# A Mamba-2 layer's convolution of x with tokens on partitions: shifted copies by DMA in place of TensorE transposes

## The chip, the cores and the metric

The kernel runs on one core of a Trainium2 chip. The metric is the device time of one execution in microseconds. A core has five engines that each work through their own instructions in order: TensorE (PE; its weight loads are listed apart as PEld), VectorE (DVE), ScalarE (ACT), GpSimd (POOL) and SyncE (SP), which here issues nearly all transfers. The transfers themselves are moved by 16 DMA engines. [...]

## The reference

The reference is a decoder trunk of two layers on 256 tokens with a width of 2048, all in float32. Layer 0 mixes tokens by latent attention (MLA), layer 1 by a state-space mixer (SSM, Mamba-2); behind each stands an MLP with a squared ReLU, 2048 to 8192 to 2048, and everything is added to the residual. The change touches the SSM mixer only, whose core is this:

```python
z, xbc, dt = jnp.split(h @ w_in, [...])            # 4096, 6144, 64 columns
xbc = silu(conv_w[0]*xbc[s-3] + conv_w[1]*xbc[s-2] + conv_w[2]*xbc[s-1] + conv_w[3]*xbc[s] + conv_b)
xs, b_in, c_in = split(xbc, [4096, 1024, 1024])    # 8 groups: x 512, B 128, C 128 columns each
# per group: cb = C B^T (256 x 256, causal); per head of 64 columns (8 heads a group):
#   y = (cb * decay(dt, head)) @ (x * dt) + d_skip * x
y = rms_norm_per_group(y * silu(z)) * norm_g
return y @ w_out                                   # 4096 to 2048
```

The convolution runs along the tokens: each column's value at token s takes the column's own values at s, s-1, s-2 and s-3 (zero before the first token), each with a weight of that column, and a bias of that column.

## The kernel before

**Products and weight units.** All large products have tokens on the output's partitions: two accumulators (tokens 0 to 127 and 128 to 255) of 512 columns in PSUM. float32 is carried as a high and a low half, and a product takes three passes. Weights stream from HBM in *units* of 128 x 1024 (512 KB): SP loads one into one of six `raw` buffers (`fetch`, L87), ScalarE makes its high half `wh` (L102), VectorE the low half `wl` (L103), four buffers each, and TensorE runs eight products with `wh` (L325, L326) and four with `wl` (L329) in `block`. `Flow.next` loads six units ahead of the one in use and converts three ahead. A *key* is two units, a *block* of the SSM layer four keys, that is 8 units, and gives 512 columns for all 256 tokens.

**Order.** TensorE's instructions stand in the order in which the program writes them. The other engines' instructions are put in order by the tile framework, which knows the waits and sets each where it expects it to be ready. At the end of each key `tick` runs the small steps that `later(n, fn)` put off by n ticks; so transposes, group products and gates fall between keys. The SSM layer's blocks come as B0, dt, B1, C0, C1 and then as `SSM_ORDER` says: x blocks (one per group), z blocks, and blocks o of the output product.

**Convolution before.** The accumulators of an x, B or C block have tokens on partitions. `conv` first copies them to SBUF (`evac`, ScalarE L1093), turns them by TensorE transposes so that columns lie on partitions and tokens along the free axis (L1070), and there a shift in time is a shifted slice: ScalarE multiplies by the last tap and adds the bias (L1076), VectorE adds the three other taps (L1079), ScalarE takes a tanh (L1081), VectorE ends the SiLU (L1082). B and C stay in that layout, which their products want. x has to come back: `back` (in `x_block`) transposes it again (L1179) and ScalarE copies it out (L1181) to `xtm`, tokens on partitions. Per x group that is 8 transposes there and 8 back.

**After the convolution.** `cb_group` makes cb (L1156 to L1161), `head` loads a broadcast row of cumulated decays (L1215, SP) and makes a head's factor on ScalarE and VectorE (L1219 to L1222); eight heads later `products` multiplies them with x (L1237), `across` adds the first half's part to the second (L1195, L1197), and the z block's `gate` (L1262 to L1276) finishes the group.

**Buffers.** All of it lies in SBUF: `xtm` six tiles, `cb` one per group, `mt` (head factors) eleven, scratch `s2` seven. GpSimd's transfers that add while they write (L199, in the MLPs only) use a scratch area for their descriptors, of the framework's default size.

## Time and profile before

| | |
|---|---|
| median of 3 runs | 2308.71 us (2308.22 to 2309.93) |
| span of the profiled execution | 2306.1 us; no other time of that execution is given, the median of the runs stands 2.6 us above it |
| TensorE busy | 2298.4 us |
| VectorE busy | 1890.2 us |
| ScalarE busy | 1419.4 us |
| GpSimd busy | 187.9 us |
| granted TensorE clock | full in all slices |
| read from HBM | 506.58 MB, 221 GB/s over the span |

How to read it: busy time is the time in which an engine had an instruction of its own under way; "x" is a count; a group's row gives its line, engine, operation, the tiles written and read, shapes, count, busy time, the mean duration of one in ns, and then the idle time of the engine ahead of these instructions with what ended it. TensorE's products overlap, so that one lasts 390 ns while they start closer together. SPq and POOLq are the queues that issue transfers; the time to landing runs from the issue to the arrival of the whole transfer.

### The profile page before, as it was taken

The numbers are of one execution on the slowest core, as the hardware profiler recorded it, in microseconds if no ns is written. First come the engines' busy times: TensorE is split into PE (matmuls) and PEld (weight loads), VectorE is DVE, ScalarE is ACT, GpSimd is POOL, SyncE is SP. The second block draws the span as 40 slices with busy tenths as digits, with TensorE's granted clock in tenths as the row PEclk, the third lists the DMA queues.
The fourth block names the chain that finished last, engine by engine and source line by source line (L and its number), as shares of the span: only waits on it lengthen the run. The fifth ranks groups of instructions, "written<-read, shape, count | busy, mean of one in ns | idle before, by whom it ended". The sixth has DMA issues, their size and how long they took to land.

```text
span 2306.1 us, 30756 instructions
## 1 busy us (share of the span) xinstructions
PE 2298.4 (100%) x11057; PEld 1911.1 (83%) x11057; DVE 1890.2 (82%) x2318; ACT 1419.4 (62%) x1995; POOL 187.9 (8%) x227
## 2 busy tenths in 40 slices
PE   9999999999999999999999999999999999999999
PEld 7888888888888888888888888888888888888887
DVE  7786697999899897678788767756989989989895
ACT  7775466566666656575577555545666656666663
POOL 1430000000000000000022001110000000000000
PEclk9999999999999999999999999999999999999999
DMA  8444677877887877665566656556687788787874
GB/s 316 148 129 155 200 233 245 262 239 250 265 243 247 267 217 241 198 211 180 169 204 207 223 181 204 186 191 201 201 257 234 250 265 250 241 268 240 250 230 161
DMA packets 152153, 510.77 MB, mean 221 GB/s; under 512 B 17152, under 2 KB 26304, under 8 KB 152000
## 3 DMA queue, kind: packets, MB, share of 16 engines
q1 hardware_dynamic: 143712, 479.37, 62.7%
q0 software_dynamic: 8064, 29.36, 7.6%
q8 instruction: 87, 1.43, 0.3%
q14 instruction: 66, 0.54, 0.1%
q10 hardware_dynamic: 224, 0.07, 0.0%
HBM read 506.58 MB, written 2.16 MB: 221 GB/s over the span
## 4 chain that ended last, share of the span: by engine, by line
PE 98%; DMA 1%; DVE 0%; ACT 0%; issue 0%; SPq 0%; POOL 0%; DVEq 0%; ACTq 0%
PE acc L325 13%; PE acc L326 13%; PE acc L329 13%; PE yp L595 9%; PE yp L596 9%; PE yp L594 9%; PE st L595 8%; PE st L596 8%; PE st L594 8%; PE sm L310 2%; PE y L1237 1%; PE acc L596 1%; PE acc L595 1%; PE acc L594 1%; PE acc L703 0%; DMA wraw<-mi 0%
## 5 line engine op out<-in xcount | busy, mean ns | idle before, releaser
L102 ACT ACTIVATE wh<-wraw 128x1024 fp32r<-128x1024 f32 (+1 forms) x818 | 860.0, 1054 | 627.6 <-PE acc L326 311.0
L103 DVE TENSOR_TENSOR wl<-wraw,wh 128x1024 fp32r<-128x1024 f32 (+1 forms) x818 | 987.9, 1220 | 265.1 <-ACT wh L102 255.0
L594 PE MATMUL yp<-wh,k 128*128 128x512 f32 x896 | 349.8, 390 | 0.0
L595 PE MATMUL yp<-wl,k 128*128 128x512 f32 x896 | 348.9, 389 | 0.5 <-DVE wl L103 0.4
L596 PE MATMUL yp<-wh,k 128*128 128x512 f32 x896 | 348.8, 389 | 0.0
L325 PE MATMUL acc<-wh,xt 128*128 128x512 f32 x704 | 280.8, 399 | 1.3 <-ACT wh L102 1.3
L326 PE MATMUL acc<-wh,xt 128*128 128x512 f32 x704 | 274.6, 390 | 0.0
L102 ACT ACTIVATE wh<-wrx 128x1024 fp32r<-128x1024 f32 x168 | 177.9, 1059 | 136.3 <-PE yp L596 108.0
L103 DVE TENSOR_TENSOR wl<-wrx,wh 128x1024 fp32r<-128x1024 f32 x168 | 204.0, 1219 | 38.5 <-ACT wh L102 38.3
L595 PEld LDWEIGHTS yp<-wl,k 128*128 128x128 f32 x896 | 168.2, 188 | 36.0 <-DVE wl L103 1.4
L596 PEld LDWEIGHTS yp<-wh,k 128*128 128x128 f32 x896 | 168.2, 188 | 35.0
L594 PEld LDWEIGHTS yp<-wh,k 128*128 128x128 f32 x896 | 168.2, 188 | 34.6
L325 PE MATMUL acc<-wh,k 128*128 128x512 f32 x496 | 196.7, 397 | 0.0
L326 PE MATMUL acc<-wh,k 128*128 128x512 f32 x496 | 193.3, 390 | 0.0
L329 PE MATMUL acc<-wl,xt 128*128 128x512 f32 x704 | 188.4, 389 | 0.0
L594 PE MATMUL st<-wh,xt 128*128 128x512 f32 x448 | 176.8, 395 | 0.0
L595 PE MATMUL st<-wl,xt 128*128 128x512 f32 x448 | 174.8, 390 | 0.0
L596 PE MATMUL st<-wh,xt 128*128 128x512 f32 x448 | 174.8, 390 | 0.0
L325 PEld LDWEIGHTS acc<-wh,xt 128*128 128x128 f32 x704 | 132.3, 188 | 29.7 <-ACT wh L102 2.8
L329 PEld LDWEIGHTS acc<-wl,xt 128*128 128x128 f32 x704 | 132.1, 188 | 27.9
L326 PEld LDWEIGHTS acc<-wh,xt 128*128 128x128 f32 x704 | 132.3, 188 | 26.9 <-issue 1.0
L199 POOL DMA_DIRECT2D wrx<-mi x56 | 48.8, 872 | 1140.3 <-DVE wl L103 1034.3
(302 smaller groups left out, 3458.8 us busy)
## 6 DMA issues: line engine op xcount, KB each, us to landing
wraw<-mi SPq DMA_DIRECT2D x256, 512.0 KB, 5.2
wraw<-mo SPq DMA_DIRECT2D x256, 512.0 KB, 5.3
wraw<-si SPq DMA_DIRECT2D x160, 512.0 KB, 4.5
wraw<-so SPq DMA_DIRECT2D x64, 512.0 KB, 4.3
wrx<-mi SPq DMA_DIRECT2D x56, 512.0 KB, 5.0
wrx<-mi POOLq DMA_DIRECT2D x56, 512.0 KB, 8.1
wraw<-wo SPq DMA_DIRECT2D x32, 512.0 KB, 3.8
wraw<-ukv SPq DMA_DIRECT2D x16, 512.0 KB, 4.1
```

The costliest lines, as they stand in the source:

```text
L102: self.last = nc.scalar.activation(h[:, v], raw[:, v], AF.Copy)
L103: nc.vector.tensor_tensor(lo[:, v], raw[:, v], h[:, v].bitcast(F32), ALU.subtract)
L199: nc.gpsimd.dma_start(st["b11"].tile, quarter(d, 1, 0), accum_op=ALU.add)
L310: self.nc.tensor.transpose(b[:, j * P:(j + 1) * P], src[:, j * P:(j + 1) * P], self.ident)
L325: nc.tensor.matmul(accs[t][:, :n], ah, wh[:, q, :], start=first and kt + q == 0, stop=False)
L326: nc.tensor.matmul(accs[t][:, :n], al, wh[:, q, :], start=False, stop=False)
L329: nc.tensor.matmul(accs[t][:, :n], lhs(kt + q, t)[0], wl[:, q, :], start=False, stop=en and q == nk - 1)
L594: nc.tensor.matmul(b, ah, wh, start=first and q == 0, stop=False)
L595: nc.tensor.matmul(b, ah, wl, start=False, stop=False)
L596: nc.tensor.matmul(b, al, wh, start=False, stop=last and q == 1)
L1237: nc.tensor.matmul(y[t][c, o], part(t)[:, c], xg[g][t][:, o], start=True, stop=True)
```

## The change

Only x's convolution, the place of four blocks, and some buffers change.

1. `x_block` no longer calls `conv`. ScalarE copies the accumulators, scaled, straight to `xtm` (tokens on partitions). `shift` then makes three copies of x that are moved down by 3, 2 and 1 tokens, that is by partitions, with SP transfers from SBUF to SBUF into `taps[0]` and `taps[1]` (128 x 3 x 512 each, one pair for all groups): for each half of the tokens 125, 126 and 127 rows of 2 KB, and for the second half 3, 2 and 1 rows that come from the first. The rows ahead of the first token are zeroed once.
2. The weights of the taps and the bias now differ along the free axis; `weights` loads them per group as a broadcast tile `cw` (128 x 2560, 1.31 MB, one buffer, from a new input `cwx`). VectorE multiplies the taps and x by them (`mult`), adds up the five terms (`total`); ScalarE's tanh and VectorE's last step as before.
3. Steps lie on ticks 0 (shift), 1 and 3 (mult), 2 and 4 (total), 4 and 5 (silu, and what follows). The two sets of transposes of x are gone.
4. `SSM_ORDER` now starts with B0, dt, C0, x0, B1, x1, C1, x2; the cb products of groups 4 to 7 move to their x blocks.
5. `cb` has five buffers, `mt` nine; `cum` takes a scratch tile; the descriptor scratch is set to 2048 bytes a partition.

```diff
+        taps = [sp.tile([P, 3, 512], F32, name=f"taps{t}") for t in range(2)]
+        self.later(3, lambda: nc.gpsimd.memset(taps[0][0:3], 0.0))
...
-            cum = sp.tile([64, S], F32, name="cum")
+            cum = self.scratch()[:64, :S]
...
-            t = sp.tile([P, 384], F32, name=f"cb{g}")
+            t = sp.tile([P, 384], F32, tag="cb", name=f"cb{g}", bufs=5)
...
         def x_block(g):
+            cw = []
+
+            def weights():
+                cw.append(sp.tile([P, 2560], F32, tag="cw", name=f"cw{g}", bufs=1))
+                nc.sync.dma_start(cw[0], d["cwx"][g])
+
+            self.later(0, weights)
             accs = self.block([("si", "x", g, q) for q in range(4)], xT)
-            ev = evac(accs)
...
-                b = self.bank(False)
-                for k in range(4):
-                    o = (k % 2) * 256 + t * P
-                    nc.tensor.transpose(b[:, k * P:(k + 1) * P], fmx[k // 2][:, o:o + P], self.ident)
...
+            x = [sp.tile([P, 512], F32, tag="xtm", name=f"xtm{g}_{t}", bufs=6) for t in range(2)]
+            th = [None, None]
+            for t in range(2):
+                nc.scalar.activation(x[t], accs[t], AF.Copy, scale=rs[t])
+
+            def shift():
+                for t in range(2):
+                    for i in range(3):
+                        m = 3 - i
+                        if t:
+                            nc.sync.dma_start(taps[1][:m, i], x[0][P - m:])
+                        nc.sync.dma_start(taps[t][m:, i], x[t][:P - m])
+
+            def mult(t):
+                flat = taps[t].rearrange("p i n -> p (i n)")
+                nc.vector.tensor_tensor(flat, flat, cw[0][:, :1536], ALU.mult)
+                nc.vector.tensor_tensor(x[t], x[t], cw[0][:, 1536:2048], ALU.mult)
+
+            def total(t):
+                for v in (taps[t][:, 2], taps[t][:, 1], taps[t][:, 0], cw[0][:, 2048:]):
+                    nc.vector.tensor_tensor(x[t], x[t], v, ALU.add)
+                th[t] = self.scratch()
+                nc.scalar.activation(th[t], x[t], AF.Tanh, scale=0.5)
+
+            def silu(t):
+                nc.vector.scalar_tensor_tensor(x[t], th[t], 1.0, x[t], ALU.add, ALU.mult)
...
-            conv(ev, 4 * g, dst, 0, back)
+            self.later(0, shift)
+            if g >= 4:
+                self.later(0, lambda: cb_group(g))
+            self.later(1, lambda: mult(0))
+            self.later(2, lambda: total(0))
+            self.later(3, lambda: mult(1))
+            self.later(4, lambda: (silu(0), total(1)))
+            self.later(5, lambda: (silu(1), ahead()))
...
-            m = sp.tile([P, 256], F32, tag="mt", name=f"mt{h}", bufs=11)
+            m = sp.tile([P, 256], F32, tag="mt", name=f"mt{h}", bufs=9)
...
-SSM_ORDER = ["x0", "x1", "x2", "z0", "x3", "z1", "x4", "z2", "o0", "x5", "z3", "x6", "z4", "o1",
+SSM_ORDER = ["B0", "d0", "C0", "x0", "B1", "x1", "C1", "x2", "z0", "x3", "z1", "x4", "z2", "o0", "x5", "z3", "x6", "z4", "o1",
              "x7", "z5", "z6", "o2a", "z7", "o2b", "o3"]
...
-    nc = bacc.Bacc("TRN2", target_bir_lowering=False, num_devices=1)
+    nc = bacc.Bacc("TRN2", target_bir_lowering=False, num_devices=1, dynamic_dma_scratch_size=2048)
```

`ahead`, not shown in full, is the unchanged second part of `back`: it queues the group's heads and computes the part that `across` adds.

More of the change, by code (lines that the diff above doesn't have):

```diff
@@ L1061, in ssm_body, with conv @@
         self.later(0, setup)
-        def conv(ev, ct, dst, lag, after):
+        taps = [sp.tile([P, 3, 512], F32, name=f"taps{t}") for t in range(2)]
+        self.later(3, lambda: nc.gpsimd.memset(taps[0][0:3], 0.0))
+        def conv(ev, ct, dst, lag):
             def half(j):
@@ L1084, in conv @@
             self.later(lag + 1, lambda: half(1))
-            if after:
-                self.later(4, lambda: after(0))
-                self.later(5, lambda: after(1))
         def evac(accs):
@@ L1101, in bc_block @@
             conv(evac(accs), (32 if name == "B" else 40) + 4 * i,
-                 lambda j: t[:, 2 * j:2 * j + 2].rearrange("p a b -> p (a b)"), 0, None)
+                 lambda j: t[:, 2 * j:2 * j + 2].rearrange("p a b -> p (a b)"), 0)
         def dt_block():
@@ L1164, in x_block @@
         def x_block(g):
-            accs = self.block([("si", "x", g, q) for q in range(4)], xT)
-            ev = evac(accs)
-            fmx = [None, None]
-            def dst(j):
-                fmx[j] = self.scratch()
-                return fmx[j]
-            def back(t):
-                if t == 0:
-                    xg[g] = []
-                b = self.bank(False)
-                for k in range(4):
-                    o = (k % 2) * 256 + t * P
-                    nc.tensor.transpose(b[:, k * P:(k + 1) * P], fmx[k // 2][:, o:o + P], self.ident)
-                x = sp.tile([P, 512], F32, tag="xtm", name=f"xtm{g}_{t}", bufs=6)
-                nc.scalar.activation(x, b, AF.Copy)
-                xg[g].append(x)
-                if t == 0:
-                    return
+            cw = []
@@ L1185, in back, with ahead @@
+            def total(t):
[5 more added lines that the diff above has]
+                nc.vector.scalar_tensor_tensor(x[t], th[t], 1.0, x[t], ALU.add, ALU.mult)
+            def ahead():
+                xg[g] = x
                 dg = self.gain_tile(d["dsk"][g])
@@ L1190, in back @@
                 xw = self.scratch()
-                nc.gpsimd.tensor_tensor(heads_of(xw), heads_of(xg[g][0]), spread(edge[:, 0]), ALU.mult)
+                nc.gpsimd.tensor_tensor(heads_of(xw), heads_of(x[0]), spread(edge[:, 0]), ALU.mult)
                 def across():
@@ L1282, in o_block @@
             return self.block([("so", 2 * i + q, nb) for q in range(2)], self.from_tiles(yT[2 * i:2 * i + 2]))
-        bc_block("B", 0)
-        dt_block()
-        bc_block("B", 1)
-        bc_block("C", 0)
-        bc_block("C", 1)
-        for g in range(GROUPS):
-            self.later(2 + g % 2 + 4 * (g // 2), lambda g=g: cb_group(g))
-        self.pump = pump
         for step in SSM_ORDER:
             kind, i = step[0], int(step[1])
-            if step == "x2":
+            if step == "C1":
                 early[0] = False
-            if kind == "x":
+            if kind in "BC":
+                bc_block(kind, i)
+                if step == "C0":
+                    for g in range(4):
+                        self.later(2 + g % 2 + 4 * (g // 2), lambda g=g: cb_group(g))
+                    self.pump = pump
+            elif kind == "d":
+                dt_block()
+            elif kind == "x":
                 x_block(i)
@@ L1425, in sequence @@
     si = lambda name, i: [add(("si", name, i, q), d["si"][q, col(name, i)]) for q in range(4)]
-    si("B", 0)
-    add(("si", "dt", 0, 0), d["sidt"], 16, 64)
-    si("B", 1), si("C", 0), si("C", 1)
     so = lambda k, nb: add(("so", k, nb), d["so"][k, nb])
@@ L1431, in sequence @@
         kind, i = step[0], int(step[1])
-        if kind in "xz":
+        if kind in "xzBC":
             si(kind, i)
+        elif kind == "d":
+            add(("si", "dt", 0, 0), d["sidt"], 16, 64)
         elif i < 3:
@@ L1506 @@
     rep = lambda v: np.broadcast_to(f(v).reshape(1, -1), (P, f(v).size))
+    taps = np.concatenate([f(ssm_conv_w)[0], f(ssm_conv_b)], 0)[:, :4096]
+    a["cwx"] = rows(taps.reshape(5, 8, 512).transpose(1, 0, 2), 2560)
     cw = f(ssm_conv_w)[0].reshape(4, 48, P).transpose(2, 1, 0).reshape(P, 192)
```

## The prediction

> **What bounds the kernel now.** I read the page's shares of engines, then its chain of waits, then stretches of the SSM layer, then the timeline around one convolution.

> ```profile
> PE 2298.4 (100%) x11057; PEld 1911.1 (83%) x11057; DVE 1890.2 (82%) x2318; ACT 1419.4 (62%) x1995; POOL 187.9 (8%) x227
> PE 98%; DMA 1%; DVE 0%; ACT 0%; issue 0%; SPq 0%; POOL 0%; DVEq 0%; ACTq 0%
> ```

> TensorE is busy for 2298.4 of 2306.1 us and the chain of waits is 98% TensorE: time is won only by taking instructions from TensorE, lost as soon as TensorE waits.

> ```profile
> 1000.00:1100.00 100.00, 100.00 (x462) 82.28 (x461) 75.03 (x126) 65.29 (x108) 0.00 (x0) 1.00 0.63 201
> 1100.00:1200.00 100.00, 99.81 (x575) 81.95 (x575) 80.71 (x124) 65.48 (x118) 16.57 (x12) 1.00 0.59 183
> 1200.00:1300.00 100.00, 100.00 (x567) 82.41 (x566) 80.29 (x114) 62.80 (x111) 19.33 (x14) 1.00 0.66 209
> 1300.00:1400.00 100.00, 100.00 (x567) 82.67 (x566) 69.31 (x92) 59.97 (x91) 14.15 (x11) 1.00 0.63 196
> ```

> In the SSM stretches (busy PE, PEld, DVE, ACT, POOL, then clock, DMA share, GB/s) TensorE never rests, its clock is full, VectorE has 20 to 30 us free per 100, the DMA engines a third.

> ```profile
> 1052.61 1.07 PE L329 MATMUL acc<-wl,xt 128*128 128x512 f32 x4
> 1053.52 0.60 PE L1070 MATMUL yp<-cst,s 128*128 128x128 f32 x4
> 1053.87 0.48 PE L325 MATMUL acc<-wh,xt 128*128 128x512 f32 x1
> ...
> 1055.80 1.07 PE L329 MATMUL acc<-wl,xt 128*128 128x512 f32 x4
> 1056.71 0.39 PE L325 MATMUL acc<-wh,xt 128*128 128x512 f32 x1
> ...
> 1058.52 1.07 PE L329 MATMUL acc<-wl,xt 128*128 128x512 f32 x4
> 1052.81 1.06 ACT L102 ACTIVATE wh<-wraw 128x1024 fp32r<-128x1024 f32 x1 [1.66 <-PE acc L326]
> ```

> A weight unit (1024 columns of raw weights, eight products with wh, four with wl) takes 1058.52 - 1055.80 = 2.72 us; its wl part begins 1058.52 - 1056.71 = 1.81 us after its start. ScalarE's split of a later unit starts at 1052.81, just when a unit's wh products end (1052.61): four wh buffers, so unit k+4 is split when unit k has used its wh.

> **The change part by part.** *Transposes.* Per x group 8 go from L1070 and 8 from L1179, in four batches of 4. With a batch the wl part begins 1055.80 - 1053.52 = 2.28 us after the stretch starts, without one 1.81: 0.47 us a batch, 32 batches, 15.0 us off TensorE, all on the path.

> *VectorE and ScalarE.*

> ```profile
> L1079 DVE SCALAR_TENSOR_TENSOR s<-sm,cst,s 128x255 f32<-128x255 f32 x38 | 18.1, 476 | 0.2
> L1082 DVE SCALAR_TENSOR_TENSOR s<-s,s 128x512 f32<-128x512 f32 x16 | 11.8, 737 | 0.0
> L183 DVE TENSOR_TENSOR wraw<-wraw,wraw 128x1024 f32<-128x1024 f32 x56 | 68.4, 1221 | 18.4 <-DMA wraw<-mi 16.9 <-DVE x L419 0.5 <-DVE wl L103 0.4
> L419 DVE TENSOR_TENSOR x<-acc,x 128x512 f32<-128x512 f32 x24 | 15.4, 683 | 7.0 <-PE acc L329 7.0
> L1076 ACT ACTIVATE s<-sm,cst 128x256 f32<-128x256 f32 x38 | 21.2, 557 | 7.7 <-DVE s L1079 5.4 <-PE sm L1070 2.2
> L1181 ACT ACTIVATE xtm<-sm 128x512 f32<-128x512 f32 x16 | 9.5, 591 | 2.8 <-PE sm L1179 2.8
> L1093 ACT ACTIVATE s<-acc,rs 128x512 f32<-128x512 f32 x24 | 15.0, 674 | 0.0
> L1195 PE MATMUL sm<-s,cb 128*128 128x512 f32 x16 | 8.2, 591 | 0.0
> L1237 PE MATMUL y<-xtm,mt 128*64 128x64 f32 x512 | 16.7, 224 | 0.0
> L103 DVE TENSOR_TENSOR wl<-wraw,wh 128x1024 fp32r<-128x1024 f32 (+1 forms) x818 | 987.9, 1220 | 265.1 <-ACT wh L102 255.0
> ```

> Gone per group: 12 x 0.48 + 2 x 0.74 = 7.2 us of VectorE. Added: two products over 1536 columns (L183 gives 1.22 for 1024, L419 0.68 for 512, so 1.8 for 1536), 10 over 512 at 0.68, 2 x 0.74: 11.9. So 4.7 more, 38 us over eight groups; the four stretches above leave 95 us of 400 free, so nothing for the amount. ScalarE loses 4 x 0.56 + 2 x 0.59 = 3.4 us per group, worth nothing as it isn't the bound. POOL gets one memset.

> *Order, buffers, scratch.* B, C and dt keep their instructions; moving B1 and C1 between x groups only spreads the conversions. cb with five buffers and mt with nine put waits on ScalarE behind a group's products; ScalarE works a few units ahead, and one unit (2.72 us) covers such a group (L1237, 16.7 / 8 = 2.1 us): nothing, or at most 2.1 us x 8 if that cover were gone. Smaller descriptor scratch concerns the POOL transfers:

> ```profile
> wrx<-mi POOLq DMA_DIRECT2D x56, 512.0 KB, 8.1
> 325.90 0.87 POOL L199 DMA_DIRECT2D wrx<-mi  x1 [14.29 <-DVE wl L103]
> 334.97 0.87 POOL L199 DMA_DIRECT2D wrx<-mi  x1 [8.20 <-DVE wl L103]
> ```

> They land in 8.1 us and the two nearest of this pass start 9.1 apart: even if only one fitted at a time, nothing.

> *Transfers.* Per group 9 shifts (125, 126, 127 rows of 2 KB for each half, and 3, 2, 1 rows) = 1.56 MB, and 1.31 MB of tap weights: 23 MB over some 650 us (160 + 64 units of 2.72, and small work), 35 GB/s beside about 200. Spread evenly that raises the DMA share from 0.63 to about 0.74 and stays hidden. They are 80 more issues on SP, between the weight loads; the next group's tap weights wait there for VectorE's last sum over the one buffer, with loads of units seven ahead (19 us) behind them: nothing; both the loads and the products over `taps` then depend on when the shifts land. That is the term that decides.

> ```profile
> wraw<-si SPq DMA_DIRECT2D x160, 512.0 KB, 4.5
> cm<-cumD SPq DMA_DIRECT2D x64, 128.0 KB, 3.8
> gb<-dsk SPq DMA_DIRECT2D x8, 256.0 KB, 2.8
> gb<-sng SPq DMA_DIRECT2D x8, 256.0 KB, 3.0
> q1 hardware_dynamic: 143712, 479.37, 62.7%
> 0.00:28.00 28.00, 25.28 (x101) 20.03 (x102) 20.23 (x35) 20.05 (x34) 1.64 (x8) 1.00 0.93 344
> L1215 SPq DMA_DIRECT2D cm<-cumD x64: 319/371/664, 1007.1 to 1447.1; - x64
> SPq L87 <- DVE wl L103: 457.5, 205, 5.3
> ```

> SP's loads wait for wl splits that free one of six raw buffers, 205 times: SP runs as far ahead as the buffers let it, so nine issues of 0.37 us cost nothing by themselves. The price of a row: 62.7% of 16 engines' 2306.1 us for 479.37 MB is 98.8 ns per 2 KB on one engine; in the first 28 us 0.93 x 16 / 344 GB/s gives 88.6 ns. The 128-row transfers of 256 KB land in 2.8 and 3.0 us, so they run on many engines (one engine alone would need 11), 8 rows each, and 2.0 us of the landing are fixed. All these transfers have row counts divisible by 16; no row here shows another count. Two ends: the 762 rows spread over 16 engines take 762 x 94 ns / 16 = 4.5 us; or a transfer is dealt in equal shares, as many up to 16 as divide its rows: 125 rows on 5 engines (25 each), 126 on 14 (9 each), 127 on a single one, always the first ones. Then the first engine gets 25 + 9 + 127 = 161 rows for the first half, 325 with the second: 15.1 and 30.6 us at 94 ns (between 88.6 and 98.8; an estimate, as no row shows SBUF to SBUF). I take the second end: 127 can't be divided evenly, and the changed program itself carries the one-row copy as 16 pieces of 32 elements, which helps only if rows are what is dealt. [...]

> Two neighbouring x groups stand 49.5 us apart:

> ```profile
> 1182.55 0.66 PE L1070 MATMUL sm<-cst,s 128*128 128x128 f32 x4
> 1232.04 0.60 PE L1070 MATMUL sm<-cst,s 128*128 128x128 f32 x4
> ```

> Now one x group, from the end of its last product (0). ScalarE has x[0] at 0.9 (0.67 each, L1093). First half landed: 0.9 + 2.0 + 15.1 = 18.0. In the changed program's order VectorE's product over taps[0] stands behind the wl split of the 5th unit after the block (unit 1's wh free at 1.81, 1.06 for wh 5, 1.22 for wl 5: reached at about 4.2) and ahead of the 6th: wl 6 is ready at 18.0 + 1.8 + 1.2 = 21.0, where TensorE wants it at 5 x 2.72 + 1.81 = 15.4. The product over taps[1] stands behind wl 7: second half landed 0.9 + 2.0 + 30.6 = 33.5, wl 8 ready at 36.5, wanted at 7 x 2.72 + 1.81 = 20.9. Small products between these units (L1195 1.0, cb, transposes of a z block), about 1.5 us, run anyway: 36.5 - 20.9 - 1.5 = 14.1 us lost per group, holding the first stall in it. Next weight load: queued behind the shifts on the first engine, at 33.5 + 1.6, needed only two units later, so nothing more. Eight groups: 113 us. A check on the first engine: between neighbouring x groups (16 units) it moves 512 KB of weights, 650 of shifts, 80 of tap weights, some 96 of others, 1338 KB at 45.9 ns = 61 us, against 49.5 - 1.9 + 14.1 = 62 for TensorE (1.9 is 15.0 / 8): about full, no more.

> Sum: 2306.1 - 15 + 113 = 2404; the runs' median 2308.71 stands 2.6 above this span: 2407.

> **The rivals.** *Spread (faster).* If shares needn't be equal, the shifts land by 0.9 + 2.0 + 4.5 = 7.4, before VectorE reaches the second product (wl 7 at 9.6); the first half lands at 5.2, 1 us late, inside 10 us of slack. All 15.0 us stay won: 2294. For it: every transfer seen is spread. It decides as long as the second half lands before about 18. *One engine each, but different ones.* The two 127-row transfers run side by side, 12 us each: wl 6 at 18, 2.8 late less 1.5 of small work: 10 to 22 us over eight groups, less 15: 2304 to 2316. *VectorE as the bound*: if a group's 4.7 us of added work all came to the path, 8 x 4.7 - 15 = +23, 2332; against it stand the 57 us of 400 that stay free. It decides only where a group's work meets ten or more us of other conversions.

> **How the numbers follow.** Equal shares on the first engines 0.80, spread 0.14, different engines 0.04, VectorE 0.02. For the first, 98.8 ns a row gives 15.7 a group and 2421, 88.6 gives 12.4 and 2393; a lone engine 20% faster (71 ns) 6.6 and 2347, one 10% slower than the slowest row about 2450: its own range 2350 to 2450. The range takes in the others below: 2290 to 2450. Faster 0.16, within 0.2% (4.6 us, what a measurement tells from no change) 0.02, slower 0.82.

> **What would show it.** L1070 x32 and no L1179; shifts of 125 to 127 rows landing after some 15 to 30 us instead of 3; VectorE waiting some 13 us ahead of each product over taps for DMA taps<-xtm; TensorE idle before L329 for wl, about 14 us in each of eight places, none outside the SSM layer; DMA share low in these stalls, as one engine works alone. Wrong if the shifts land in 3 to 7 us and TensorE stays whole, or if the lone engine's row costs much other than 94 ns.

## The result, and the profile after

The changed kernel takes 2478.3 us (median of 5 runs, 2475.6 to 2480.3), the kernel before 2308.7 us (5 runs, 2307.5 to 2309.9). The ratio is 1.0735, 95% interval 1.0722 to 1.0748: slower by 170 us, where the prediction said slower by 98 and at most 2450 us. The profiled execution spans 2476.0 us.

The page of the changed kernel: busy time by engine, the chain of waits by engine, the queue of SP.

```profile
PE 2337.5 (94%) x10929; PEld 1926.4 (78%) x10929; DVE 1925.5 (78%) x2318; ACT 1388.7 (56%) x1947; POOL 192.7 (8%) x228
...
q1 hardware_dynamic: 151568, 502.34, 62.0%
...
PE 74%; DMA 10%; DVE 6%; SPq 4%; issue 4%; ACT 3%; POOL 1%; DVEq 0%; ACTq 0%; POOLq 0%
```

TensorE has 128 instructions less, and yet it is busy 39 us longer than before (2337.5 against 2298.4) and idle 138.5 us of the span (it was 7.7). The chain is no longer TensorE's: 10% of it are transfers, 6% VectorE, 8% SP's issues and what shows no cause.

The four SSM stretches that the prediction showed (busy PE, PEld, DVE, ACT, POOL, then granted clock, DMA share, GB/s):

```profile
1000.00:1100.00 100.00, 88.09 (x379) 71.11 (x378) 65.14 (x106) 49.62 (x85) 1.35 (x1) 0.93 0.60 189
1100.00:1200.00 100.00, 70.45 (x332) 56.09 (x331) 56.28 (x74) 33.65 (x56) 6.96 (x4) 0.85 0.50 162
1200.00:1300.00 100.00, 79.51 (x424) 62.42 (x423) 69.61 (x88) 43.94 (x82) 21.96 (x14) 0.88 0.59 184
1300.00:1400.00 100.00, 75.17 (x347) 58.21 (x346) 62.63 (x83) 42.56 (x74) 9.20 (x7) 0.88 0.57 182
```

TensorE rests 12 to 30 us in each hundred, the clock is below full, and the DMA share has gone down although there is more to move: the transfer engines wait for one of their own. Of the 29.7 us from the first to the last row of the first group's copies, exactly one 2-KB row was under way for 20.1 us, 84 ns each.

The waits of the SSM layer (950 to 1850 us; engine and line, what it waited for, us in all, times, longest), and the timelines of VectorE and TensorE in the first x group:

```profile
DVE taps L1188 <- DMA taps<-xtm: 157.5, 14, 14.4
...
ACT wh L102 <- DMA wraw<-si: 103.3, 6, 25.3
...
PE acc L329 <- DVE wl L103: 101.5, 24, 10.7
...
ACT mt L1243 <- DMA cm<-cumD: 40.3, 14, 6.6
...
PE sm L1212 <- DVE k L300: 24.9, 4, 6.9
```

```profile
1046.80 1.76 DVE L1188 TENSOR_TENSOR taps<-taps,cw 128x1536 f32<-128x1536 f32 x1 [12.78 <-DMA taps<-xtm]
...
1061.40 1.76 DVE L1188 TENSOR_TENSOR taps<-taps,cw 128x1536 f32<-128x1536 f32 x1 [9.97 <-DMA taps<-xtm]
```

```profile
1044.06 0.39 PE L326 MATMUL acc<-wh,xt 128*128 128x512 f32 x1
1049.75 2.08 PE L329 MATMUL acc<-wl,xt 128*128 128x512 f32 x4 [5.30 <-DVE wl L103]
...
1064.35 2.08 PE L329 MATMUL acc<-wl,xt 128*128 128x512 f32 x4 [6.61 <-DVE wl L103]
```

The first copy is issued at 1029.6. VectorE's products over `taps` start 17.2 and 31.8 us later; in all eight groups it is 16.6 to 17.7 and 31.3 to 32.4. TensorE stands before the `wl` products of two units, as forecast. The four products of such a unit then take 2.08 us together in place of 1.07, at half the granted clock (0.50 from 1049.75 to 1051.83 us). The other rows are not in the forecast: ScalarE waits 103 us for weights and 40.3 us for the heads' rows, and TensorE 24.9 us at L1212, the product across the chunk.

### The profile page after: what moved, and what is told of

It reads as the page before. It is cut to its first block, busy times and chain, and to the rows that moved or that the text cites. A ratio compares the mean times of both kernels' runs of the same rounds, so it can differ in the third digit from the quotient of the medians.

```text
span 2476.0 us, 30571 instructions
## 1 busy us (share of the span) xinstructions
PE 2337.5 (94%) x10929; PEld 1926.4 (78%) x10929; DVE 1925.5 (78%) x2318; ACT 1388.7 (56%) x1947; POOL 192.7 (8%) x228
## 4 chain that ended last, share of the span: by engine, by line
PE 74%; DMA 10%; DVE 6%; SPq 4%; issue 4%; ACT 3%; POOL 1%; DVEq 0%; ACTq 0%; POOLq 0%
PE yp L595 8%; PE yp L596 8%; PE yp L594 8%; PE acc L325 8%; PE acc L326 8%; PE acc L329 8%; PE st L595 6%; PE st L596 6%; PE st L594 6%; DMA taps<-xtm 6%; DVE wl L103 3%; SPq L1183 3%; DMA wraw<-mi 2%; DMA cm<-cumD 2%; PE sm L310 1%
## 5 line engine op out<-in xcount | busy, mean ns | idle before, releaser
L102 ACT ACTIVATE wh<-wraw 128x1024 fp32r<-128x1024 f32 (+1 forms) x818 | 855.6, 1052 | 678.7 <-PE acc L326 246.6
L103 DVE TENSOR_TENSOR wl<-wraw,wh 128x1024 fp32r<-128x1024 f32 (+1 forms) x818 | 990.1, 1224 | 214.0 <-ACT wh L102 205.8
L329 PE MATMUL acc<-wl,xt 128*128 128x512 f32 x704 | 205.2, 416 | 99.2 <-DVE wl L103 99.2
L325 PE MATMUL acc<-wh,xt 128*128 128x512 f32 x704 | 292.6, 416 | 1.6 <-ACT wh L102 1.6
L326 PE MATMUL acc<-wh,xt 128*128 128x512 f32 x704 | 285.3, 405 | 0.0
L102 ACT ACTIVATE wh<-wrx 128x1024 fp32r<-128x1024 f32 x168 | 177.8, 1059 | 136.5 <-PE yp L596 107.4
L329 PEld LDWEIGHTS acc<-wl,xt 128*128 128x128 f32 x704 | 139.7, 202 | 136.7 <-DVE wl L103 107.6
L103 DVE TENSOR_TENSOR wl<-wrx,wh 128x1024 fp32r<-128x1024 f32 x168 | 204.1, 1219 | 36.9 <-ACT wh L102 36.7
L325 PE MATMUL acc<-wh,k 128*128 128x512 f32 x496 | 200.5, 404 | 0.0
L326 PE MATMUL acc<-wh,k 128*128 128x512 f32 x496 | 196.1, 395 | 0.0
L325 PEld LDWEIGHTS acc<-wh,xt 128*128 128x128 f32 x704 | 140.2, 199 | 35.4 <-ACT wh L102 5.2
L1188 DVE TENSOR_TENSOR taps<-taps,cw 128x1536 f32<-128x1536 f32 x16 | 28.1, 1758 | 174.9 <-DMA taps<-xtm 157.5
L326 PEld LDWEIGHTS acc<-wh,xt 128*128 128x128 f32 x704 | 139.8, 199 | 30.9 <-issue 1.8
## 6 DMA issues: line engine op xcount, KB each, us to landing
wraw<-mi SPq DMA_DIRECT2D x256, 512.0 KB
wraw<-mo SPq DMA_DIRECT2D x256, 512.0 KB
wraw<-si SPq DMA_DIRECT2D x160, 512.0 KB
wraw<-so SPq DMA_DIRECT2D x64, 512.0 KB
wrx<-mi SPq DMA_DIRECT2D x56, 512.0 KB
wrx<-mi POOLq DMA_DIRECT2D x56, 512.0 KB, 8.1
wraw<-wo SPq DMA_DIRECT2D x32, 512.0 KB
```

Of the source, the lines that this page charges most:

```text
L102: self.last = nc.scalar.activation(h[:, v], raw[:, v], AF.Copy)
L103: nc.vector.tensor_tensor(lo[:, v], raw[:, v], h[:, v].bitcast(F32), ALU.subtract)
L325: nc.tensor.matmul(accs[t][:, :n], ah, wh[:, q, :], start=first and kt + q == 0, stop=False)
L326: nc.tensor.matmul(accs[t][:, :n], al, wh[:, q, :], start=False, stop=False)
L329: nc.tensor.matmul(accs[t][:, :n], lhs(kt + q, t)[0], wl[:, q, :], start=False, stop=en and q == nk - 1)
L1188: nc.vector.tensor_tensor(flat, flat, cw[0][:, :1536], ALU.mult)
```

## The experiments

**The dealing of the rows.** The same bytes, in copies whose row counts 16 divides, plus a rest:

```diff
-                        nc.sync.dma_start(taps[t][m:, i], x[t][:P - m])
+                        for a, b in ((0, 112), (112, P - m)):
+                            nc.sync.dma_start(taps[t][m + a:m + b, i], x[t][a:b])
```

2311.5 us (10 runs, 2309.4 to 2316.4), ratio 1.0014 [1.0004, 1.0023]. 167 of the 170 us are gone with nothing changed but how the copies are cut. Its busy times and the waits of its SSM layer:

```profile
PE 2289.2 (99%) x10929; PEld 1900.2 (82%) x10929; DVE 1924.1 (83%) x2318; ACT 1394.4 (60%) x1947; POOL 193.5 (8%) x228
```

```profile
ACT mt L1244 <- DMA cm<-cumD: 28.1, 15, 4.9
...
PE sm L1213 <- DVE k L300: 12.5, 4, 4.8
...
ACT wh L102 <- DMA wraw<-si: 8.4, 4, 3.6
```

No wait at L329 is left, and the products over `taps` wait for nothing worth a row. It is still 17 us over the 2294 of the forecast's "spread" rival; what is left is the wait at the product across the chunk (L1213 here), taken up further down.

Two other counts, each as one transfer: 120 rows and, in the same way, 124 rows (`taps` is zeroed once ahead of them).

```diff
-                        nc.sync.dma_start(taps[t][m:, i], x[t][:P - m])
+                        nc.sync.dma_start(taps[t][m:m + 120, i], x[t][:120])
```

> Every shift copies 120 rows in one transfer from the same offsets; the last 5 to 7 rows of each shift are left out. Theory A: 15 engines with 8 rows each, so as with the split ones: no wait worth naming at the product over taps, about 2294 us. Theory B: 5% fewer bytes and still the same offsets, so about 2470 us.

2326.0 us (one run). The products over `taps` start 5.7 to 8.5 and 11.2 to 15.3 us after the first issue, much as with the split copies (6.2 to 8.5 and 12.4 to 15.5). The time is 32 us over what was expected; 21.7 us of waiting at the product across the chunk are the largest part of it. So neither the shift by one to three partitions nor a copy within SBUF is slow by itself: the count decides.

> Every shift copies 124 rows in one transfer; the last 1 to 3 rows of each shift are left out. Theory A: 124 is dealt to 4 engines, 31 rows each, and always the same four: 93 rows for the first half, 186 for both, at 94 ns 8.7 and 17.5 us. The product over taps[0] starts some 11 us after the first issue, that over taps[1] some 20 us after it (17.2 and 31.8 in the changed kernel); TensorE loses at most 1 to 3 us a group: about 2300 to 2315 us. If 124 rows were spread like 120: 2294 us. Theory B: about 2475 us.

2401.0 us (one run). The products start 11.4 to 13.1 and 20.9 to 24.0 us after the first issue, near what four engines would give (expected 11 and 20). The records of the rows say so too: of the 20.1 us from the first to the last row of the first group, exactly four were under way for 14.2. Yet the time is 86 us or more over what was expected from that. Its waits:

```profile
DVE taps L1188 <- DMA taps<-xtm: 70.7, 9, 9.8
...
ACT wh L102 <- DMA wraw<-si: 56.0, 6, 15.6
...
PE acc L329 <- DVE wl L103: 42.9, 24, 6.3
ACT mt L1243 <- DMA cm<-cumD: 41.0, 12, 7.6
...
PE sm L1212 <- DVE k L300: 23.6, 4, 6.4
```

The landing was foreseen and the time was not. ScalarE waits 56 us for weights: it seems that what is queued behind the copies costs something that the forecast had left out.

**The half clock.** TensorE runs 140 us of the changed kernel at half clock, in 20 stretches of 3.4 to 10.2 us. Here it is kept busy with products that nobody reads, in the units where it waits (`spare` is a bank):

```diff
+                more = self.warm.pop(self.flow.at, 0)
+                if more:
+                    spare = self.bank(False)
+                for _ in range(more):
+                    nc.tensor.matmul(spare, lhs(kt, 0)[0], wh[:, 0, :], start=True, stop=True)
...
+            self.warm[self.flow.at + 6], self.warm[self.flow.at + 8] = 20, 26
```

> The changed kernel with products that nobody reads, 20 of 512 columns in unit 6 after each x block and 26 in unit 8, between the wh and the wl products, where TensorE waits for wl; 4.5 and 5.9 us of added TensorE work in each of eight groups, 83 us in all. Theory C (part of the lost time is the clock at half speed after each idle stretch): the half-clock stretches behind these two places go, of 140 us at half clock some 35 to 45 stay behind the waits of the across product, and the time falls by 25 to 45 us although work was added: about 2433 to 2453 us. Theory D (the time is set by the landing of the shifts alone): unchanged or longer, 2478 us and above.

2478.0 us (4 runs, 2477.3 to 2480.0), ratio 1.0732 [1.0714, 1.0749]: no change, though the time at half clock falls to 58 us and the idle time before the `wl` products to 36.9 us. The added work only took the place of waiting, so TensorE's clock in these units does not set the time. What does set it, this run doesn't show; the next ones ask.

**Who waits for the copies.** The next three take away VectorE's dependence on the copies and leave the copies on the queue. The first lets it work on the tap weights in place of `taps`:

```diff
-                flat = taps[t].rearrange("p i n -> p (i n)")
-                nc.vector.tensor_tensor(flat, flat, cw[0][:, :1536], ALU.mult)
+                flat = cw[0][:, :1536]
+                nc.vector.tensor_tensor(flat, flat, flat, ALU.mult)
...
-                for v in (taps[t][:, 2], taps[t][:, 1], taps[t][:, 0], cw[0][:, 2048:]):
+                for v in (cw[0][:, :512], cw[0][:, 512:1024], cw[0][:, 1024:1536], cw[0][:, 2048:]):
```

> The changed kernel with its whole copies, issued and landing as they do there, but VectorE no longer reads them: the product and the three sums take the tap weights in place of taps (the result leaves out the convolution's shifted rows). VectorE keeps its instructions and no longer waits for the copies. Of the 170 us that the changed kernel lost, the prediction put 113 on VectorE's wait for the copies and nothing on what is queued behind them. By that theory (F) TensorE is whole but for what is left over: 2293 to 2315 us. Rival theory (G): the weights and the rows for the heads that stand behind the copies on the first engine hold the path by themselves, whoever reads the copies: the neighbouring x groups still stand at least 61 us apart (the first engine's own work), five pairs x 13 us over 2293, and what lands late of weights comes on top: 2360 to 2430 us, with ScalarE waiting for DMA wraw and cm rows and TensorE ahead of its wl products.

2484.6 us, as slow as the changed kernel, but it tells nothing: VectorE's next product overwrites `x` in place, the copies read `x`, and so it waited for them as before.

```profile
DVE xtm L1189 <- DMA taps<-xtm: 166.3, 15, 15.9
```

The second takes a constant tile as the source of the copies.

> The run before it on this question replaced VectorE's reading of the copies' destination, but its product overwrites x in place and the copies read x, so VectorE waited for them all the same (166 us). Here the copies have the same shapes, queue and destination, but read a constant tile (the first 125 rows still read x, so that they are issued at the same time); VectorE again takes the tap weights in place of taps (the result leaves out the convolution's shifted rows). Now nothing that VectorE or TensorE does waits for the copies. Theory F, VectorE's wait for the copies is the cause: 2293 to 2320 us. Theory G, what is queued behind the copies on the first engine (weights, cumulative rows, tap weights) holds the path by itself: neighbouring x groups still stand 61 us or more apart, five pairs x 13 us over 2293, and more where weights land late: 2360 us or more. Between them, each has a part of it.

2460.9 us, which tells little as well. Without a dependence on `x` the program's order moved the copies: 64 issues come between 907.7 and 1178.0 us, most of them far ahead of their groups. It shows only that TensorE can be idle 135 us over these copies while VectorE waits for them 46 us, and not 157. The third leaves the copies exactly where they are, from `x` to `taps`, and VectorE writes neither:

```diff
+                nc.vector.tensor_tensor(cw[0][:, 1536:2048], x[t], cw[0][:, 1536:2048], ALU.mult)
...
+                w = cw[0][:, 1536:2048]
+                for v in (cw[0][:, 1024:1536], cw[0][:, 512:1024], cw[0][:, :512], cw[0][:, 2048:]):
+                    nc.vector.tensor_tensor(w, w, v, ALU.add)
```

> The run with a constant tile as the source told little of this question, since the copies no longer waited for x and 52 of 72 were issued ahead of their groups. Here the copies read x and write taps, in the places of the changed kernel, and nobody waits for them: VectorE works on the tap weights in place of taps and x, and leaves x as the products made it (the result leaves out the convolution). Theory F, VectorE's wait for the copies is what costs: no L329 waits, 2293 to 2320 us. Theory G, the weights and cumulative rows queued behind the copies on the first engine cost by themselves: ScalarE waits for them, the cycle of neighbouring x groups stays at 61 us or more, 2360 us or more. Between: each has a part, and the difference to 2478 is VectorE's part.

2427.4 us (2 runs, 2426.1 and 2428.8), ratio 1.0514 [1.0493, 1.0535]. Its waits, and one place on ScalarE's and on TensorE's timeline:

```profile
ACT wh L102 <- DMA wraw<-si: 128.7, 16, 23.1
...
PE acc L325 <- ACT wh L102: 87.4, 8, 13.8
```

```profile
1061.05 1.06 ACT L102 ACTIVATE wh<-wraw 128x1024 fp32r<-128x1024 f32 x1 [20.24 <-DMA wraw<-si]
```

```profile
1051.74 1.07 PE L329 MATMUL acc<-wl,xt 128*128 128x512 f32 x4
1062.16 0.79 PE L325 MATMUL acc<-wh,xt 128*128 128x512 f32 x1 [9.35 <-ACT wh L102]
```

This settles that the queue costs by itself. No instruction waits for the copies except for one of 1.7 us, the stalls at `wl` are gone, and TensorE waits in eight places for `wh`, 87.4 us, because the weights land behind the copies: here at 1061.0, 33.8 us after the first copy was issued at 1027.3. Against the 2294 that the change would give with nothing in the way, the queue alone costs 134 us, TensorE's half clock after these waits included; against the split copies, which keep a wait at the product across the chunk as this run does, it is 116. VectorE's wait adds the other 51.

The records of the single rows in the changed kernel show this queue at work. Behind the first group's copies SP issues four weight loads of 128 rows. Of these, 480 rows, that is fifteen sixteenths, start between 1051.8 and 1059.5 us; the next one starts at 1060.9, when the last row of the copies has ended, and from there they go one by one, 0.16 us apart. So the loads are held by the one engine that still has copies to do. SP is late with them too (see the last section), but not by enough. In the run in which nobody waits, the first 120 weight rows were in at 1051.9; ScalarE's 1.06 us added, that gives 1053 (an estimate), where TensorE wanted them at 1052.8 and got them at 1062.2.

**The copies from another queue.** Whole copies, all nine issued by POOL:

```diff
-                            nc.sync.dma_start(taps[1][:m, i], x[0][P - m:])
-                        nc.sync.dma_start(taps[t][m:, i], x[t][:P - m])
+                            nc.gpsimd.dma_start(taps[1][:m, i], x[0][P - m:])
+                        nc.gpsimd.dma_start(taps[t][m:, i], x[t][:P - m])
```

> The changed kernel with its whole copies (125, 126 and 127 rows, nothing split), issued from POOL's queue in place of SP's. Theory K, dealing by divisors belongs to any queue: 127 rows stay on one engine, the copies land after 12 us or more each, and the time is 2380 to 2480 (the weights of SP's queue get their turn between them, so that they may be less late than before). Theory L, a queue of POOL deals rows of any count to all engines: the copies land within 5 us, no wait ahead of the products over taps, no row of SP's queue held behind, 2294 to 2312 us; what may be left over is POOL's own time for making the descriptors. [...]

2353.5 us (4 runs, 2349.3 to 2355.4), ratio 1.0191 [1.0176, 1.0206]: between the two theories. The tile's view and the waits:

```profile
L1184 POOL DMA_DIRECT2D taps<-xtm x48: 530/541/647, 1027.3 to 1511.6; - x48
...
DMA to landing us min/median/max: 5.8/8.6/12.2
```

```profile
DVE taps L1188 <- DMA taps<-xtm: 46.4, 8, 6.9
...
PE sm L1212 <- DVE k L300: 25.2, 6, 7.3
POOL taps L1184 <- DMA taps<-xtm: 21.7, 8, 3.5
...
PE acc L329 <- DVE wl L103: 12.3, 8, 3.5
```

The first group's first product over `taps` starts 9.5 us after the first issue (16.6 to 17.7 from SP), so this queue doesn't leave 127 rows to one engine: its first group's rows go mostly two to a packet, with up to 16 packets under way at once and a single one for only 1.6 us. In this the run is on theory L's side. But a landing of 8.6 us is no 5, and POOL's last copies of a group wait for earlier ones to land (21.7 us in eight places). Whether that wait comes from the smaller descriptor scratch was not tried.

**The other parts.** The two sizes alone, in the kernel before (`mt` with nine buffers, descriptor scratch of 2048):

> The kernel before with two sizes of the change alone: mt with nine buffers in place of eleven, descriptor scratch of 2048 in place of the default. The prediction costs both at nothing (2308.7, within 0.2%). Rival: nine buffers make ScalarE wait behind a group's products, up to 2.1 us x 8 = 17 us: 2312 to 2326.

2308.0 us (10 runs, 2307.2 to 2309.6), ratio 0.9997 [0.9988, 1.0007]: nothing. The new order, with `cb` in five buffers, `cum` in a scratch tile and the small descriptor scratch:

> The kernel before with the new order alone: B, C and dt blocks between the first x blocks, cb with five buffers, cum in a scratch tile, descriptor scratch of 2048; x with its transposes and mt with eleven buffers as before. The prediction costs all of it at nothing: 2308.7, within 0.2%. Rival: the order is what brings the late evictions ahead of the product across the chunk, which the run with split copies showed (17 us over the forecast for spread copies): 2313 to 2326.

2311.5 us (10 runs, 2310.2 to 2312.7), ratio 1.0012 [1.0002, 1.0022]: 3 us, within the 0.2% that the prediction called no change, but above zero.

**What the split copies leave over.** In the chain of waits of the split kernel, just ahead of TensorE's longest wait:

```profile
1165.34 5.88 DMA cm<-cumD
...
1171.24 0.40 ACT mt L1244
1171.64 0.49 ACT k L299
...
1172.16 0.70 DVE k L300
...
1172.99 2.05 PE sm L1213 x2
```

ScalarE waits for a head's row `cm` until 1171.2 and only behind L1244 begins the eviction (L299 at 1171.64, then VectorE's L300 at 1172.16) that frees the bank for L1213 (1172.99). Two cures, the rows from ScalarE's own queue, and the product two units later:

```diff
-            nc.sync.dma_start(cm, cumD[h:h + 1].to_broadcast([P, S]))
+            nc.scalar.dma_start(cm, cumD[h:h + 1].to_broadcast([P, S]))
```

> The copies split in 112 rows and 13 to 15 (2311 us, 17 us over what the forecast gives for copies that are spread), and the 64 loads of the cumulative rows cm issued from ScalarE's queue in place of SP's, where they stand behind up to 15 issues of copies. Theory H, the 17 us come from cm rows that land late, so that ScalarE holds back the eviction ahead of the product across the chunk: cm no longer waits for SP, the waits at that product (12.5 us) go, and the time is 2294 to 2300. Rival I, they come from the order (B and C blocks between the x blocks, fewer buffers) or from VectorE's backlog: the waits at that product stay, 2308 to 2312. Rival J, 64 issues on ScalarE cost it so much that the splits come late: above 2312.

2309.6 us (10 runs, 2306.1 to 2312.7), ratio 1.0005 [0.9995, 1.0014]; the wait at L1213 is 9.9 us, and ScalarE still waits 30.8 us for rows. Theory H falls: taking the rows off SP's queue does not take these waits away.

```diff
-                self.later(1, across)
+                self.later(3, across)
```

> The copies split, and the product across the chunk put two units later. With the split copies TensorE waits 12.5 us in four places at that product, for a bank that VectorE's eviction (L300) frees late. Theory M, it is a matter of place: two units (5.4 us) later the bank is free, TensorE has no wait, and the time is 2294 to 2300 us, the forecast for copies that are spread. Theory N, ScalarE and VectorE are behind at these places whatever is asked of them: the wait moves to another bank or to the products after it, 2306 to 2312 us.

2301.6 us (7 runs, 2300.5 to 2303.7), ratio 0.9972 [0.9961, 0.9983]. The wait at the product is gone, and this version beats the kernel before by 0.3%. It is a matter of place, theory M, though 1.6 us above M's range and 7.6 above its best time: 6.0 us of idle time remain, mostly before L310, with 7 us at half clock behind the longest.

> Both: the product across the chunk two units later and the cumulative rows loaded from ScalarE's queue. If place alone settles it (M), the rows make no difference: 2294 to 2300 us, within 2 us of the run beside it. If the late rows are what keeps ScalarE behind (H) beside the place, this run is the faster by 3 us or more.

2305.8 us (10 runs, 2303.5 to 2309.4), ratio 0.9990 [0.9980, 1.0000]: the rows from ScalarE's queue gain nothing on top. They cost 4 us, where theory M expected no more than 2 either way; the cause was not looked for.

## Why the prediction was right and wrong

*Transposes* (15.0 us). With the copies split and the product across moved, TensorE is busy 2289.1 us. Less some 3 us lost to the half clock (6.8 us of it, the last section) that is 2286, some 13 below the 2298.4 before. The term holds, 2 us smaller.

*VectorE and ScalarE, order, buffers, scratch* (nothing). Right within 0.2%: VectorE is busy 35 us longer (38 expected) and this is hidden; sizes 0.9997; order 1.0012. What the sum left out is the product across the chunk: with split copies TensorE waits 12.5 us there, and in the changed kernel 24.9 us. That product has a bank behind ScalarE's queue, and the prediction named no such place.

*The dealing of rows* (first engine, 161 and 325 rows, at 94 ns). Right in the landing and in the one engine for 127 rows: one row was under way for 20.1 of 29.7 us. That it is the first of the engines, and that 125 rows go to 5 and 126 to 14, no run shows: the records name no engine. The second half's landing was put at 32.6 us after the first issue, and VectorE's second product began at 31.3 to 32.4; the first at 17.1, and it was 16.6 to 17.7. A row took 84 ns while under way, under the 88.6 to 98.8 assumed, but 29.7 us for 325 rows are 91 ns with what lies between, so the sum of the landing came out. 112 + 15 rows undo it, and so do 120; 124 rows land as from four engines. VectorE's second product after the first issue, at 11.2 to 15.3, 20.9 to 24.0 and 31.3 to 32.4 us for 120, 124 and 127 rows, agrees with equal shares.

*VectorE's wait, 14.1 us per group, 113 in all.* In the trace it looks right: 101.5 us of idle time before L329, two stalls a group, mostly of 5 to 7 us, where the prediction had one net figure. But it is not what this wait is worth. Taken away by itself, it gives back 51 us.

*"Next weight load: queued behind the shifts on the first engine, at 33.5 + 1.6, needed only two units later, so nothing more."* This is the step that failed, and with it the check "about full, no more". By the prediction's own numbers the weights land at 35.1 - 0.9 = 34.2 us after the first issue; measured 33.8. The two units of room were counted from a TensorE already held up by VectorE. With that wait gone TensorE wants these weights 25.5 us after the first issue (1052.8 - 1027.3) and stands still 9.35 us. I treated two limits as one, taking the later of them, and they add in part. The check should have raised the alarm: 61 us of work on the first engine against 47.6 us for TensorE (49.5 - 1.9) is a limit of its own. It came out at 62.3, 63.7, 65.9 and 65.9 us between the first issues of the first five x groups when nobody waits for the copies. With VectorE's wait these distances are 63.8, 69.1, 74.6 and 73.9. But that limit is not all of it. From the fifth to the sixth group there are twice as many weights, 1930 KB in all on the first engine, which makes 89 us by the prediction's price (an estimate). With split copies this distance is 96.3 us, and with the copies on the queue and nobody waiting 113.9: there the first engine isn't full, and the late landing costs 17.6 us all the same. Why the two waits add is argued and not shown: six raw buffers are freed by `wl` splits (SP's loads wait 451.1 us for them between 950 and 1850 us of the changed kernel), so a VectorE that stands still also keeps SP from issuing loads, and a full queue loses time that it can't make up.

*The half clock* was not in the sum. It makes TensorE 54 us busier (2337.5 against 2298.4 - 15.0), but removing more than half of it gave no time back.

*SP's issues* ("nine issues of 0.37 us cost nothing by themselves") were mis-sized: the nine take 11.7 to 12.6 us a group, and the first weight load behind them another 8.3 to 9.1. By the estimate above they cost little beside the first engine's queue; a run that frees SP alone was not made.

The direction, the place and, as far as the runs show it, the dealing of the rows were right. The path was not: the loss was put wholly on VectorE's wait, while the queued weights cost more than it by themselves. Against the saving of 15 the effect was 185 us, and not 113. A run in which VectorE waits for the copies and no weights are held up was not made, so how much that wait would cost alone stays open. (The prediction's 2421 us for the dearest row is 2419 by its own terms, which changes nothing.)

## What to carry to other kernels

A copy shifted by one to three partitions had 125 to 127 rows here, and from SP's queue 127 were left to one engine (one row under way for 20.1 of 29.7 us): cut it at a multiple of 16 and send the rest apart (112 rows and the rest took 2311.5 us in place of 2478.3). When one transfer sits on one engine, add up that engine's whole load per cycle, weights included, and compare it with the cycle without any stall (62.3 to 65.9 us here, against 47.6): if it is above, it is a bound of its own, and a wait that overlaps with it in the sum is no cover for it. Even below that, ask when the weights behind the copies are wanted by an engine that nothing else has held up. An experiment that takes a wait away has to look for the second dependence (here a tile overwritten in place) and for where the tile framework then puts the work.

## What the runs showed that I had not expected

SP itself is held by these copies. Its timeline in the changed kernel's first group (L1184 the large copies, L1183 the copies of one to three rows):

```profile
1029.61 2.50 SPq L1184 DMA_DIRECT2D taps<-xtm  x3
1032.16 6.00 SPq L1183 DMA_DIRECT2D taps<-xtm  x1
...
1041.54 0.68 SPq L1184 DMA_DIRECT2D taps<-xtm  x1
1042.63 30.75 SPq L87 DMA_DIRECT2D wraw<-si  x8
```

A three-row copy needs 6.00 us to issue when it stands behind the 127-row one (0.7 us with split copies), so the first weight load of the group is begun 13 us after the first copy. With split copies SP needs 10 to 11 us for the 15 issues, with none so long. The weight load itself is then held as well; its issues between 1000 and 1300 us (min/median/max in ns):

```profile
L87 SPq DMA_DIRECT2D wraw<-si x70: 327/328/8933, 1002.3 to 1299.5; - x70
```

In each of the eight groups the load behind the copies takes 8.3 to 9.1 us to issue; with split copies no load takes more than 1.7. In the first group no row of a weight load starts between 1032.1 and 1051.8 us. What holds SP was not tested.

How long TensorE may rest before its clock halves is not one number here. In the changed kernel each of the 20 stretches at half clock starts within an idle time of 2.9 to 10.7 us, or up to 1.5 us behind it. An idle stretch of 2.3 us was followed by 6.8 us at half clock (copies split, product moved), one of 1.9 us (changed kernel) and one of 3.2 us (copies split, rows from ScalarE's queue) by none.

VectorE's sums of two SBUF tiles take about twice as long in the split kernel while POOL's tensor operations run. VectorE's and POOL's timelines:

```profile
1149.47 3.21 DVE L1194 TENSOR_TENSOR xtm<-xtm,taps 128x512 f32<-128x512 f32 x2
1152.71 1.66 DVE L1194 TENSOR_TENSOR xtm<-xtm,cw 128x512 f32<-128x512 f32 x1
```

```profile
1147.17 3.51 POOL L1293 TENSOR_TENSOR xtm<-s,xtm 128x512 f32<-128x512 f32 x2 [38.92 <-DVE s L1283]
1150.64 1.49 POOL L1209 TENSOR_TENSOR s<-xtm,edge 128x512 f32<-128x512 f32 x1
1152.10 3.43 POOL L1265 TENSOR_TENSOR xtm<-xtm,gb 128x512 f32<-128x512 f32 x2
```

About 1.6 us a sum, where the median of these sums is 0.68. The two coincide in time; a run that keeps them apart was not made.
